# The first MLP product in written order with P3 in P2's banks, a new order of the out-projection chunks, and a norm by token rows

## The chip, the cores and the metric

One NeuronCore of a Trainium2 chip runs the whole program. The metric is the device time of one execution in microseconds (us), median of several runs.

## The reference

A decoder trunk of two layers over 1040 tokens (16 meta tokens and 1024 of the input), model width 1024, MLP width 4096, all in float32. Layer A: norm, stick-breaking attention, residual, norm, MLP with squared ReLU, residual. Then one shared key and value projection, and layer B with differential attention and the same kind of MLP. The part that the change touches is this, once in each layer:

```python
def rmsnorm(x, g):
    xf = x.astype(jnp.float32)
    y = xf * lax.rsqrt(jnp.mean(xf * xf, axis=-1, keepdims=True) + EPS)
    return (y * g.astype(jnp.float32)).astype(x.dtype)

def squared_relu_mlp(x, g, w_in, w_out):
    h = rmsnorm(x, g)
    return jnp.square(jax.nn.relu(h @ w_in)) @ w_out
...
            h = h + merge_heads(o) @ a_w_o[i]
...
        h = h + squared_relu_mlp(h, mlp_norm_g[layer], mlp_w_in[layer], mlp_w_out[layer])
```

## The kernel before

Activations stand with the model width on the partitions and tokens along the free dimension. Every float32 matmul is made of three: an operand is split by a cast (ScalarE) and a subtraction (VectorE) into a high and a low part, and high x high, high x low and low x high are added up in PSUM.

`mlp_stage` (line 732) runs once per layer (tag a, tag b; a letter at the end of a tile's name). It does four things.

**Out-projection and residual.** `step(m, v, k0)` makes row block m of the attention's output projection for one chunk v of tokens (tiles `opa`, weights `woa`), adds it to the residual (`hs[0]`, `hs[1]`, which are the two halves of the tokens, named `h0a` and `h1a`), squares it, and adds the square to the chunk's `acc`. The three chunks have 400, 384 and 256 tokens in layer a; the first lies in half 0, the last in half 1, the middle one in both. Blocks 0 to 2 come first for all chunks, then blocks 3 to 7 chunk by chunk, in the order 0, 1, 2.

**Norm.** `normed(v)` sums a chunk's `acc` over the partitions with one matmul by a matrix of ones (`rsa`), takes the root (ScalarE) and the RECIPROCAL (VectorE) on 128 rows that all hold the same, and scales the eight blocks.

**First product.** It is a seven-product scheme on 2 x 2 blocks. `ops7(c)` makes the seven operand blocks of half c (`put` is a cast and a subtraction of 128x1040 each), `w_split(u, i)` the seven weight blocks of unit u from raw weights `mwsa` (one sum, three differences s6, s7, s3, then cast and subtraction of 128x512 each). There are 16 units. `unit` runs P1 to P7, each of 24 matmuls of 260 columns (256 in layer b), 12 for each half; unit 0 is done in two parts, half 0 and then half 1. P1, P6, P7 and P4 use the PSUM buffer q1 in turn, P5 and P3 add up in q2, P2 has q3. Between products, sums are copied or added out (`u1a` to `u7a`, `ya`), squared ReLUs are taken, and the results are stored in `u_d`. Buffers come from a ring of four, three per unit, so q3 of a unit is the buffer that was q2 in the unit before.

```python
    PROD1 = (1, 5, 6, 2, 7, 3, 4)
...
                    q = {1: q1, 6: q1, 7: q1, 4: q1, 5: q2, 3: q2, 2: q3}[i]
...
                                mm(q[:, c, :nn], w[:, k], X7[c][i][:, y, k], k == 0 and wi == 0 and i in (1, 5, 2),
                                   k == 3 and wi == 2, skip_group_check=True)
...
                    elif i == 3:
                        tt(s(y12), b2, s(y12), ALU.add)
```

**Second product.** Seven passes of 16 steps read `u_d` and the output weights (tiles `moa`); each step makes two pairs of high and low parts (`waa`, `wba`) in the ring `wop`, which the weight pairs of the first product share. Behind it, between the layers, the stretch goes on with the projections of attention b (`bpj`), whose weights POOL scales (`bws`, line 1272).

What sets the order: a scheduler reorders the written instructions of every engine by its own simulation of their times, within the dependences, unless an instruction is pinned (`tc.keep_in_program_order`). So the order in which TensorE runs the products is not the written one. Line 159 is the matmul helper `mm`, 162 the transpose helper `tr`, 99, 105, 113 and 117 the helpers for casts, activations, two-operand and scalar-and-two-operand instructions.

Of the kernel before, what the change touches and what calls it, by code (L numbers as in the profile page):

```python
# [17 lines left out]
P = 128  # L18
# [60 lines left out]
def kernel(ctx: ExitStack, tc: tile.TileContext, inp, out):  # L79
# [78 lines left out]
    def mm(o, l, r, start, stop, **kw):  # L158
        nc.tensor.matmul(o, lhsT=l, rhs=r, start=start, stop=stop, **kw)  # L159

    def tr(o, i, ident):
        nc.tensor.transpose(out=o, in_=i, identity=ident)  # L162
# [565 lines left out]
    PROD1 = (1, 5, 6, 2, 7, 3, 4)  # L728
# [3 lines left out]
    def mlp_stage(li, WO, wo_src, wo_scale, O, views, kf, gcol, base, close_w, chunk_done, epilogue):  # L732
# [7 lines left out]
        st_h1, st_tp, st_h0 = ExitStack(), ExitStack(), ExitStack()  # L740
        hs = [None, pool(f"h1{tag}", stack=st_h1).tile([P, KT, half], F32, name=f"h1{tag}")]
        tp = pool(f"tp{tag}", stack=st_tp)
        accs = [tp.tile([P, 400], F32, tag="acc", bufs=3, name=f"acc{tag}_{c}") for c in range(3)]
        hs[0] = pool(f"h0{tag}", stack=st_h0).tile([P, KT, half], F32, name=f"h0{tag}")
# [7 lines left out]
        def wop(nm):  # L752
            return mw.tile([P, 2, 520], F32R, tag="wop", bufs=10, name=nm)
# [51 lines left out]

        def wo_load(m):
            ws = raw(f"wos{tag}_{m}").rearrange("p a b -> p (a b)").rearrange("p (k n) -> p k n", n=P)
            nc.sync.dma_start(out=ws, in_=wo_src[:, m * P:(m + 1) * P].rearrange("(k q) n -> q k n", q=P))
            W = []
            for k4 in range(2):  # L810
                w = wop(f"wo{tag}_{m}_{k4}")
                h, l = (w[:, i, :512].rearrange("p (k n) -> p k n", n=P) for i in range(2))
# [18 lines left out]
        def ops7(c):  # L831
# [4 lines left out]
            def tmp(nm):  # L836
                return wop(nm).bitcast(F32).rearrange("p a b -> p (a b)")[:, :4 * nn].rearrange("p (k n) -> p k n", n=nn)

            t3, t4 = (B12, B21) if not c else (tmp(f"t3{tag}"), tmp(f"t4{tag}"))
            return [lambda: put(c, 1, B11), lambda: tt(B11, B12, B11, ALU.subtract), lambda: put(c, 5, B11),  # L840
                    lambda: tt(t3, B22, B12, ALU.subtract), lambda: put(c, 3, B22), lambda: tt(B22, B22, B11, ALU.subtract),
                    lambda: put(c, 6, B22), lambda: put(c, 2, B21), lambda: tt(t4, B21, B22, ALU.subtract),
                    lambda: put(c, 7, t3), lambda: put(c, 4, t4)]
# [3 lines left out]

        for v in views:
            load_hs(v, 0, NMF)
        for m in range(NMF, KT):  # L850
            if m == NMF + 2:
                load_hs(views[0], NMF, KT)
            wo_load(m)
        for v in views[1:]:
            load_hs(v, NMF, KT)
# [3 lines left out]
        close_w()  # L859
        st_x = ExitStack()  # L860
        fa = pool(f"fa{tag}", stack=st_x, side="right")
        mc = pool(f"mc{tag}", stack=st_x, side="right")
# [32 lines left out]
        def unit(u, parts, more):  # L895
# [3 lines left out]
            U = {i: mc.tile([P, half], F32, tag="u", bufs=12, name=f"u{i}{tag}_{u}") for i in (1, 3, 5, 2, 4, 6, 7)}  # L899
            y12 = mc.tile([P, half], F32, tag="u", bufs=12, name=f"y{tag}_{u}")  # L900
            for pi, cs in enumerate(parts):
# [10 lines left out]

                for i in PROD1:
                    q = {1: q1, 6: q1, 7: q1, 4: q1, 5: q2, 3: q2, 2: q3}[i]
                    h, l = wops[u, i]
                    for k in range(4):
                        for wi, (w, y) in enumerate(((h, 0), (h, 1), (l, 0))):
                            for c in cs:
                                mm(q[:, c, :nn], w[:, k], X7[c][i][:, y, k], k == 0 and wi == 0 and i in (1, 5, 2),
                                   k == 3 and wi == 2, skip_group_check=True)  # L920
                    if i == 1:
                        acopy(s(U[1]), b1)
                    elif i == 6:
                        acopy(s(y12), b1)
                    elif i == 2:
                        tt(s(U[1]), b3, s(U[1]), ALU.add)
                        relu2(s(U[1]), s(U[1]))
                    elif i == 7:
                        acopy(s(U[3]), b1)
                        tt(s(U[3]), b2, s(U[3]), ALU.add)  # L930
                        relu2(s(U[3]), s(U[3]))
                    elif i == 3:
                        tt(s(y12), b2, s(y12), ALU.add)
                        relu2(s(y12), s(y12))
                        tt(s(U[5]), s(y12), s(U[1]), ALU.subtract)
                        tt(s(U[7]), s(U[3]), s(y12), ALU.subtract)
                        tt(s(U[6]), s(U[3]), s(U[5]), ALU.subtract)
                    elif i == 4:
                        relu2(s(U[2]), b1)
                        tt(s(U[4]), s(U[2]), s(U[6]), ALU.subtract)  # L940
                    if last_part and u + 1 < NPAIR:
                        w_split(u + 1, i)
                    more()
# [9 lines left out]
        x0, x1 = None, None  # L953
        for ci, v in enumerate(views):
            for m in range(NMF, KT):
                step(m, v, 0)
                if ci and m == NMF:
                    chunk_done(hs, ci - 1, ps1, srow)
                    normed(views[ci - 1])
                    if ci == 2:  # L960
                        w_load(0)
                        w_load(1)
                        x0, x1 = xact(0, 3, f"x0{tag}"), xact(1, 3, f"x1{tag}")
                        x2 = fa.tile([P, 2, 4, nn], F32R, name=f"x2{tag}")
# [595 lines left out]
```

## Time and profile before

| | |
|---|---|
| median of 3 runs | 2813.18 us (2811.96 to 2815.2) |
| profiled execution | 2817.75 us |
| its span | 2816.0 us |
| mean granted clock of TensorE | 0.979 |
| busy share: TensorE, VectorE, ScalarE, POOL | 94%, 71%, 54%, 12% |
| moved by DMA | 341.79 MB, 121 GB/s on average |

MLP a's first product runs from about 752 to 1109 us of the span and its second until 1440; in layer b they lie between 2134 and 2500, and from there to the end. Matmuls are pipelined: the records overlap, each shows about 0.28 us at 256 columns while one starts every 0.12 us. So a duration of a group of matmuls is read from the starts, not from the sum of the records. "[0.68 <-ACT u3a L99]" at a row's end means that the engine was idle for 0.68 us and that ScalarE's write of `u3a` (line 99) ended it.

### The profile page before, as it was taken

The numbers are of one execution on the slowest core, as the hardware profiler recorded it, in microseconds if no ns is written. First come the engines' busy times: TensorE is split into PE (matmuls) and PEld (weight loads), VectorE is DVE, ScalarE is ACT, GpSimd is POOL, SyncE is SP. The second block draws the span as 40 slices with busy tenths as digits, with TensorE's granted clock in tenths as the row PEclk, the third lists the DMA queues.
The fourth block names the chain that finished last, engine by engine and source line by source line (L and its number), as shares of the span: only waits on it lengthen the run. The fifth ranks groups of instructions, "written<-read, shape, count | busy, mean of one in ns | idle before, by whom it ended". The sixth has DMA issues, their size and how long they took to land.

```text
span 2816.0 us, 50084 instructions
## 1 busy us (share of the span) xinstructions
PE 2639.5 (94%) x18328; PEld 2487.6 (88%) x18328; DVE 1993.7 (71%) x3972; ACT 1513.0 (54%) x3543; POOL 335.2 (12%) x807
## 2 busy tenths in 40 slices
PE   7999999989799999899999999999897999999999
PEld 7889899978799999899999989999897999987887
DVE  6988999886955555665768878888768555457654
ACT  4666666664444444344556667667545444434443
POOL 2211111000000000000034334433000000000000
PEclk9999999999899999999999999999999999999999
DMA  7332233346143447733431112123352343495343
GB/s 209 93 82 78 78 80 80 105 137 188 44 148 128 141 144 271 249 100 103 133 86 47 39 53 57 50 58 113 102 172 94 131 142 134 159 340 165 94 109 116
DMA packets 298712, 341.79 MB, mean 121 GB/s; under 512 B 32537, under 2 KB 209346, under 8 KB 298466
## 3 DMA queue, kind: packets, MB, share of 16 engines
q1 hardware_dynamic: 289106, 334.32, 38.7%
q10 hardware_dynamic: 9360, 4.26, 0.6%
q8 instruction: 145, 2.38, 0.4%
q14 instruction: 101, 0.83, 0.1%
HBM read 206.99 MB, written 97.28 MB: 108 GB/s over the span
## 4 chain that ended last, share of the span: by engine, by line
PE 64%; DVE 11%; DMA 5%; ACT 4%; issue 2%; POOL 1%; SPq 1%; DVEq 0%; ACTq 0%; POOLq 0%
PE mia L159 11%; PE mib L159 11%; PE moa L159 10%; PE mob L159 9%; PE bpj L159 8%; PE sc_b L159 2%; PE pj L159 2%; DVE kp L494 2%; PE opb L159 2%; PE avb L159 2%; PE opa L159 1%; PE av L159 1%; PE ofb L159 1%; DVE wt L113 1%; PE ofa L159 1%
## 5 line engine op out<-in xcount | busy, mean ns | idle before, releaser
L159 PE MATMUL moa<-wba,waa 128*128 128x260 f32 x2688 | 326.7, 284 | 8.1 <-ACT wba L99 7.3
L159 PEld LDWEIGHTS moa<-wba,waa 128*128 128x128 f32 x2688 | 325.4, 189 | 9.1 <-ACT wba L99 7.7
L159 PE MATMUL mob<-wab,wbb 128*128 128x512 f32 x1344 | 316.1, 396 | 9.3 <-ACT wbb L99 7.0
L159 PEld LDWEIGHTS mob<-wab,wbb 128*128 128x128 f32 x1344 | 253.6, 189 | 70.5 <-ACT wbb L99 7.9
L159 PE MATMUL pj<-xa,wh 128*128 128x400 f32 (+2 forms) x1152 | 293.7, 334 | 8.0 <-DVE rsa L664 5.8
L159 PE MATMUL bpj<-bwh,xb 128*128 128x384 f32 x1024 | 283.0, 345 | 4.7 <-ACT k L99 3.7
L159 PEld LDWEIGHTS pj<-xa,wh 128*128 128x128 f32 x1152 | 204.0, 194 | 10.0 <-POOL ws L121 6.2
L159 PEld LDWEIGHTS bpj<-bwh,xb 128*128 128x128 f32 x1024 | 187.6, 190 | 8.2 <-ACT k L99 5.8
L494 DVE TENSOR_TENSOR_SCAN kp<-kp 128x144 f32<-128x144 f32 (+7 forms) x128 | 185.3, 1452 | 11.7 <-ACT kp L105 11.0
L159 PE MATMUL pj<-xa,wl 128*128 128x384 f32 (+2 forms) x576 | 191.5, 333 | 0.1
L159 PE MATMUL bpj<-bwl,xb 128*128 128x384 f32 x512 | 174.5, 341 | 0.0
L1272 POOL TENSOR_SCALAR bws<-bws,gains 128x128 f32<-128x128 f32 (+1 forms) x128 | 69.4, 548 | 824.5 <-DMA bws<-in_kv_w_dram 776.7
L105 ACT ACTIVATE w<-sc,rsa 128x392 f32<-128x392 f32 (+4 forms) x224 | 121.7, 544 | 33.6 <-PE sc L159 31.9
L105 ACT ACTIVATE kp<-sc,rsa 128x392 f32<-128x392 f32 (+4 forms) x224 | 120.3, 539 | 12.9 <-DVE w L113 12.8
L113 DVE TENSOR_TENSOR wt<-pt,wt 128x512 fp32r<-128x512 f32 x160 | 106.4, 681 | 23.4 <-ACT wt L99 22.8
L1331 DVE TENSOR_REDUCE mxb<-sc_b 128x1 f32<-128x144 f32 (+6 forms) x224 | 109.6, 503 | 18.0 <-PE sc_b L159 16.6
L99 ACT CAST wt<-pt 128x512 fp32r<-128x512 f32 x160 | 90.3, 587 | 56.9 <-PE av L159 51.6
L159 PE MATMUL av<-wt,v 128*128 128x256 f32 x640 | 109.7, 294 | 7.6 <-DVE wt L113 5.1
L159 PEld LDWEIGHTS pj<-xa,wl 128*128 128x128 f32 x576 | 111.5, 194 | 0.8 <-DVE wl L113 0.3
L113 DVE TENSOR_TENSOR w<-w,kp 128x143 f32<-128x143 f32 (+7 forms) x128 | 110.5, 868 | 2.0
L162 PE MATMUL pt<-cst,w 128*128 128x128 f32 x640 | 105.6, 279 | 5.3 <-DVE zm L113 2.7
L159 PEld LDWEIGHTS av<-wt,v 128*128 128x128 f32 x640 | 91.2, 193 | 12.0 <-DVE wt L113 7.0
(478 smaller groups left out, 7447.8 us busy)
## 6 DMA issues: line engine op xcount, KB each, us to landing
ba<-u_d SPq DMA_DIRECT2D x112, 260.0 KB, 2.7
bb<-u_d SPq DMA_DIRECT2D x112, 256.0 KB, 2.8
mwsa<-in_mlp_w_in_dram SPq DMA_DIRECT2D x32, 512.0 KB, 3.8
mwsb<-in_mlp_w_in_dram SPq DMA_DIRECT2D x32, 512.0 KB, 3.9
o_d<-oh SPq DMA_DIRECT2D x52, 256.0 KB, 2.5
ws<-in_a_w_qkv_dram SPq DMA_DIRECT2D x24, 512.0 KB, 4.2
qb<-q SPq DMA_DIRECT2D x128, 64.0 KB, 2.0
a12a<-in_mlp_w_out_dram SPq DMA_DIRECT2D x16, 512.0 KB, 4.1
```

Source lines behind the costliest of these rows:

```text
L99: nc.scalar.copy(out=o, in_=i)
L105: nc.scalar.activation(out=o, in_=i, func=func, **kw)
L113: nc.vector.tensor_tensor(out=o, in0=a, in1=b, op=op)
L159: nc.tensor.matmul(o, lhsT=l, rhs=r, start=start, stop=stop, **kw)
L162: nc.tensor.transpose(out=o, in_=i, identity=ident)
L494: nc.vector.tensor_tensor_scan(out=rv, data0=rv, data1=rv, initial=1.0, op0=ALU.mult, op1=ALU.bypass)
L1272: nc.gpsimd.tensor_scalar(out=ws[:, s], in0=ws[:, s], scalar1=gains[:, gc + k:gc + k + 1], scalar2=1.0, op0=ALU.mult, op1=ALU.mult)
L1331: nc.vector.tensor_reduce(out=mx[:, j:j + 1], in_=ps[:, 0], axis=AX.X, op=ALU.max, negate=True)
```

## The change

1. `mm`, `tr` return their instruction, and `pin` keeps one in program order. The first matmul of every product is pinned. In units 1 to 15 the order is 1, 5, 6, 2, 7, 3, 4 as before in the text; in unit 0 it is 1, 2, 5, 3, 6, 7, 4, and half 1 comes first.
2. P3 starts its own sum in q3, after P2's was read out, so `y12` takes two additions: P5 from q2, P3 from q3.
3. The chunks go in the order 1, 2, 0. Half 1's blocks are made during chunk 0; chunk 0's norm and half 0's blocks are written inside unit 0's first part (`second`).
4. The raw weights of units 0 and 1 are loaded and the seven splits of unit 0 are written ahead of the chunks.
5. The norm works on token rows: `rms_of` sums with `acc` as weights, so that 128 tokens stand on the partitions and each group of 128 tokens is a column; the root and RECIPROCAL act on at most four columns; `normed` transposes the factors, broadcast to 128, into PSUM (`rba`), from where the scaling reads them.
6. Memory: `wop` has 8 buffers instead of 10 and moves to a pool that lives to the end of the second product, and the weights of the out-projection have a ring of their own with five buffers, which some operand blocks use afterwards; `u` has 10 instead of 12. The weights of attention b take the place of `wop`.

```diff
-        def normed(v):
+        def rms_of(v):
 
             c, off, n = v
-            r = tp.tile([P, 400], F32, tag="r", bufs=1, name=f"r{tag}{c}")[:, :n]
             ps = ps1(f"rs{tag}{c}")
-            mm(ps[:, :n], ones, accs[c][:, :n], True, True)
-            act(r, ps[:, :n], AF.Sqrt, scale=1.0 / D, bias=epst)
-            nc.vector.reciprocal(out=r, in_=r)
+            r = tp.tile([P, 4], F32, tag="r", bufs=3, name=f"r{tag}{c}")
+            nf, rem = divmod(n, P)
+            for i in range(nf + (rem > 0)):
+                w = P if i < nf else rem
+                ins = mm(ps[:w, 2 * i:2 * i + 2], accs[c][:, P * i:P * i + w], ones[:, 0:2], i == 0, i == nf + (rem > 0) - 1,
+                         skip_group_check=True)
+                if i == 0:
+                    pin(ins)
+            for w, i, k in [(P, 0, nf)] + ([(rem, nf, 1)] if rem else []):
+                act(r[:w, i:i + k], ps[:w, 2 * i:2 * (i + k):2], AF.Sqrt, scale=1.0 / D, bias=epst[:w])
+                nc.vector.reciprocal(out=r[:w, i:i + k], in_=r[:w, i:i + k])
+            return r
+
+        def normed(v, r):
+
+            c, off, n = v
+            ps = ps1(f"rb{tag}{c}")
+            for o in range(0, n, P):
+                w = min(P, n - o)
+                ins = tr(ps[:, o:o + w], r[:w, o // P:o // P + 1].to_broadcast([w, P]), idf[:w, :w])
+                if o == 0:
+                    pin(ins)
             for x, a, b, w in pieces(v):
                 for k in range(KT):
                     hv = hs[x][:, k, a:a + w]
-                    stt(hv, hv, gains[:, gcol + k:gcol + k + 1], r[:, b:b + w], ALU.mult, ALU.mult)
+                    stt(hv, hv, gains[:, gcol + k:gcol + k + 1], ps[:, b:b + w], ALU.mult, ALU.mult)
...
-                for i in PROD1:
-                    q = {1: q1, 6: q1, 7: q1, 4: q1, 5: q2, 3: q2, 2: q3}[i]
+                done = set()
+                for pn, i in enumerate(prods):
+                    q = {1: q1, 6: q1, 7: q1, 4: q1, 5: q2, 3: q3, 2: q3}[i]
...
-                                mm(q[:, c, :nn], w[:, k], X7[c][i][:, y, k], k == 0 and wi == 0 and i in (1, 5, 2),
-                                   k == 3 and wi == 2, skip_group_check=True)
+                                ins = mm(q[:, c, :nn], w[:, k], X7[c][i][:, y, k], k == 0 and wi == 0 and i in (1, 5, 2, 3),
+                                         k == 3 and wi == 2, skip_group_check=True)
+                                if k == 0 and wi == 0 and c == cs[0]:
+                                    pin(ins)
...
+                    if now(6, 5):
+                        tt(s(y12), b2, s(y12), ALU.add)
...
-                    elif i == 3:
-                        tt(s(y12), b2, s(y12), ALU.add)
+                    if now(6, 5, 3):
+                        tt(s(y12), b3, s(y12), ALU.add)
...
+        w_load(0)
+        w_load(1)
+        for i in PROD1:
+            w_split(0, i)
+
+        for ci, v in enumerate(order):
             for m in range(NMF, KT):
                 step(m, v, 0)
                 if ci and m == NMF:
-                    chunk_done(hs, ci - 1, ps1, srow)
-                    normed(views[ci - 1])
+                    chunk_done(hs, order[ci - 1], ps1, srow)
+                    r = rms_of(order[ci - 1])
+                if ci and m == NMF + 1:
+                    normed(order[ci - 1], r)
                     if ci == 2:
...
+        def second(pi, pn):
+
+            nonlocal todo
+            if pi:
+                return
+            if pn == 1:
+                late["r"] = rms_of(order[2])
+            elif pn == 2:
+                normed(order[2], late["r"])
...
+            elif pn > 2:
+                work(3)
+
+        unit(0, ((1,), (0,)), PROD0, second)
```

How it moves instructions, at three places. First **TensorE in unit 3 of layer a**, at the ends of its last products. A row is a line, the operation, the PSUM tile (`mia_3_0_0` is unit 3's q1, `_1` q2, `_2` q3) and the operands (`w7a_3` is the weight block of P7). Before:

```order
L159 MATMUL mia_3_0_0_10005<-x5a_9343,w7a_3_9918 128x260
L159 MATMUL mia_3_0_0_10005<-x2a_9052,w4a_3_9983 128x260
...
L159 MATMUL mia_3_0_0_10005<-x5a_9343,w4a_3_9983 128x260
L159 MATMUL mia_3_0_1_10006<-x1a_9051,w3a_3_9953 128x260
...
L159 MATMUL mia_3_0_1_10006<-x4a_9238,w3a_3_9953 128x260
L159 MATMUL mia_4_0_2_10243<-x1a_9051,w2a_4_10121 128x260
```

And now:

```order
L159 MATMUL mia_3_0_2_10027<-xaa_9113,w2a_3_9905 128x260
L159 MATMUL mia_3_0_0_10025<-y7a_9311,w7a_3_9938 128x260
...
L159 MATMUL mia_3_0_0_10025<-x7a_9218,w7a_3_9938 128x260
L159 MATMUL mia_3_0_2_10027<-y3a_9309,w3a_3_9973 128x260
...
L159 MATMUL mia_3_0_2_10027<-xba_9114,w3a_3_9973 128x260
L159 MATMUL mia_3_0_0_10025<-xda_9315,w4a_3_10003 128x260
...
L159 MATMUL mia_3_0_0_10025<-x4a_9219,w4a_3_10003 128x260
L159 MATMUL mia_4_0_0_10262<-xca_9308,w1a_4_10053 128x260
```

P4 no longer comes directly behind P7, nor P2 of the next unit behind P3; P3 writes q3, and unit 4 begins with its P1.

Second **TensorE at the handover of layer a**, from the last chunk's out-projection into unit 0. Before:

```order
L159 MATMUL opa_2_7_9152<-oa2_7586,woa_7_0_8522 128x256 x12
L159 MATMUL opa_2_7_9152<-oa2_7586,woa_7_1_8525 128x256 x12
L159 MATMUL rsa2_9199<-acca_2_8478,ones_66 128x256
L159 MATMUL mia_0_0_0_9253<-x0a_9050,w1a_0_9186 128x260 x12
L159 MATMUL mia_0_0_1_9254<-x0a_9050,w5a_0_9193 128x260 x12
L159 MATMUL mia_0_0_2_9255<-x1a_9051,w2a_0_9218 128x260 x12
L159 MATMUL mia_0_0_0_9253<-x0a_9050,w6a_0_9215 128x260 x12
L159 MATMUL mia_0_1_0_9381<-x3a_9237,w1a_0_9186 128x260 x12
L159 MATMUL mia_0_0_0_9253<-x1a_9051,w7a_0_9223 128x260 x12
L159 MATMUL mia_0_1_1_9382<-x3a_9237,w5a_0_9193 128x260
```

And now:

```order
L159 MATMUL opa_0_7_9185<-oa0_7055,woa_7_8522 128x400 x24
L159 MATMUL mia_0_0_0_9241<-xaa_9113,w1a_0_8656 128x260 x12
L159 MATMUL mia_0_0_2_9243<-xaa_9113,w2a_0_8668 128x260 x12
L159 MATMUL rsa0_9272<-ones_66,acca_0_8479 128x2 x3
L159 MATMUL rsa0_9272<-ones_66,acca_0_8479 16x2
L159 MATMUL mia_0_0_1_9242<-xaa_9113,w5a_0_8660 128x260 x12
L162 MATMUL rba0_9294<-cst_60,ra0_9273 128x128 x3
L162 MATMUL rba0_9294<-cst_60,ra0_9273 128x16
L159 MATMUL mia_0_0_2_9243<-xba_9114,w3a_0_8678 128x260 x12
L159 MATMUL mia_0_0_0_9241<-xba_9114,w6a_0_8665 128x260 x12
L159 MATMUL mia_0_0_0_9241<-x7a_9218,w7a_0_8673 128x260 x12
L159 MATMUL mia_0_0_0_9241<-x4a_9219,w4a_0_8681 128x260 x12
```

The norm of the last chunk stood ahead of the first product and now stands inside it, behind P2; its transposes (`rba0`) stand behind P5.

Third **VectorE in the out-projection of layer a, now**, after chunk 1's last row block but one:

```order
L113 TENSOR_TENSOR woa_7_8522<-wosa_7_8520,woa_7_8522 128x512 x2
L113 TENSOR_TENSOR w1a_0_8656<-mwsa_0_0_8648,w1a_0_8656 128x512
L113 TENSOR_TENSOR mwsa_0_0_8648<-mwsa_0_0_8648,mwsa_0_1_8650 128x4x128
...
L113 TENSOR_TENSOR w4a_0_8681<-mwsa_0_1_8650,w4a_0_8681 128x512
L113 TENSOR_TENSOR mwsa_1_0_8652<-mwsa_1_0_8652,mwsa_1_1_8654 128x4x128
L113 TENSOR_TENSOR w1a_1_9413<-mwsa_1_0_8652,w1a_1_9413 128x512
L113 TENSOR_TENSOR acca_1_8480<-acca_1_8480,sqa_1_7_0_8851 128x120
L113 TENSOR_TENSOR acca_1_8480<-acca_1_8480,sqa_1_7_1_8856 128x264
```

The splits of the weights of unit 0 and the first of unit 1 stand ahead of the last additions into chunk 1's `acca_1`, on which its norm waits; before, they stood behind all of that chunk's additions.

## Rows read from the trace of the kernel before

**Rows 1.** The page: the span, and TensorE's busy time and share.
```profile
span 2816.0 us, 50084 instructions
...
PE 2639.5 (94%) x18328; PEld 2487.6 (88%) x18328; DVE 1993.7 (71%) x3972; ACT 1513.0 (54%) x3543; POOL 335.2 (12%) x807
```

**Rows 2.** Stretches: busy time (instructions) by engine, granted clock, DMA share, GB/s.
```profile
740.00:752.00 12.00, 0.95 (x3) 0.84 (x3) 12.00 (x16) 3.59 (x4) 0.00 (x0) 0.50 0.19 59
751.71:776.31 24.60, 23.20 (x171) 22.20 (x169) 24.38 (x35) 16.86 (x34) 0.00 (x0) 0.93 0.10 33
800.00:1075.00 275.00, 258.11 (x2104) 253.37 (x2104) 145.12 (x222) 133.23 (x226) 0.00 (x0) 1.00 0.40 138
1125.00:1140.00 15.00, 9.21 (x77) 8.99 (x75) 4.08 (x7) 0.00 (x0) 0.00 (x0) 0.92 1.07 377
1260.00:1310.00 50.00, 50.00 (x418) 50.00 (x417) 31.01 (x53) 20.68 (x36) 0.00 (x0) 1.00 0.38 103
2133.67:2161.50 27.83, 23.29 (x169) 22.01 (x168) 27.39 (x40) 15.57 (x30) 0.00 (x0) 0.93 0.15 48
```

**Rows 3.** Waits of TensorE, 752 to 1100: us in total, times, longest.
```profile
PE mia L159 <- DVE ya L113: 11.0, 13, 1.6
PE mia L159 <- ACT u3a L99: 8.2, 12, 0.7
```

**Rows 4.** Waits of TensorE, 2134 to 2490, same columns.
```profile
PE mib L159 <- DVE yb L113: 11.4, 13, 2.0
```

**Rows 5.** Timeline of TensorE in layer a: start, duration, instruction [wait and releaser].
```profile
859.74 0.28 PE L159 MATMUL mia<-x5a,w7a 128*128 128x260 f32 x1
860.71 0.39 PE L159 MATMUL mia<-x2a,w4a 128*128 128x260 f32 x1 [0.68 <-ACT u3a L99]
...
867.52 0.39 PE L159 MATMUL mia<-x1a,w2a 128*128 128x260 f32 x1 [0.79 <-DVE ya L113]
...
870.52 0.28 PE L159 MATMUL mia<-x0a,w1a 128*128 128x260 f32 x1
...
873.39 0.28 PE L159 MATMUL mia<-x0a,w6a 128*128 128x260 f32 x1
...
882.84 0.39 PE L159 MATMUL mia<-x2a,w4a 128*128 128x260 f32 x1 [0.68 <-ACT u3a L99]
```

**Rows 6.** Timeline of ScalarE in the same unit.
```profile
860.06 0.59 ACT L99 COPY u3a<-mia 128x520 f32<-128x520 f32 x1 [2.26 <-PE mia L159]
```

**Rows 7.** Timeline of TensorE at the two handovers.
```profile
751.05 1.22 PE L159 MATMUL rsa<-acca,ones 128*128 128x256 f32 x2 [15.33 <-DVE acca L113]
...
2133.04 1.19 PE L159 MATMUL rsb<-accb,ones 128*128 128x256 f32 x2 [11.67 <-DVE accb L113]
```

**Rows 8.** Timeline of TensorE in layer b: the fourth product of two units.
```profile
2441.28 0.39 PE L159 MATMUL mib<-x2b,w4b 128*128 128x256 f32 x1 [0.68 <-ACT u3b L99]
...
2463.10 0.39 PE L159 MATMUL mib<-x2b,w4b 128*128 128x256 f32 x1 [0.68 <-ACT u3b L99]
```

**Rows 9.** Instructions of VectorE by line, 800 to 1075: busy us, mean ns | idle before.
```profile
L113 DVE TENSOR_TENSOR u7a<-u3a,ya 128x520 f32<-128x520 f32 x13 | 9.0, 694 | 0.0
L113 DVE TENSOR_TENSOR u1a<-mia,u1a 128x520 f32<-128x520 f32 x13 | 9.0, 693 | 1.4 <-issue 1.4
```

**Rows 10.** Timeline of TensorE, then of VectorE, in the out-projection of layer a.
```profile
691.66 8.83 PE L159 MATMUL opa<-oa,woa 128*128 128x400 f32 x48 [0.84 <-ACT woa L99]
...
723.95 11.78 PE L159 MATMUL opa<-oa,woa 128*128 128x256 f32 x96
...
700.92 0.69 DVE L113 TENSOR_TENSOR mwsa<-mwsa,mwsa 128x512 f32<-128x512 f32 x1 [0.53 <-DMA mwsa<-in_mlp_w_in_dram]
```

**Rows 11.** Timeline of POOL, then of TensorE, between MLP a and attention b.
```profile
1438.06 0.48 POOL L1272 TENSOR_SCALAR bws<-bws,gains 128x256 f32<-128x256 f32 x1 [0.75 <-DMA bws<-in_kv_w_dram]
...
1445.16 3.38 PE L159 MATMUL rsx<-ones,accx 128*128 128x2 f32 x16 [5.41 <-DVE accx L113]
1449.05 0.42 PE L159 MATMUL bpj<-bwh,xm 128*48 128x256 f32 x1 [0.51 <-DVE nx L117]
```

More of the change, by code (lines that the diff above doesn't have):

```diff
@@ L158, in mm, with pin @@
     def mm(o, l, r, start, stop, **kw):
-        nc.tensor.matmul(o, lhsT=l, rhs=r, start=start, stop=stop, **kw)
+        return nc.tensor.matmul(o, lhsT=l, rhs=r, start=start, stop=stop, **kw)
     def tr(o, i, ident):
-        nc.tensor.transpose(out=o, in_=i, identity=ident)
+        return nc.tensor.transpose(out=o, in_=i, identity=ident)
+    def pin(ins):
+        tc.keep_in_program_order(ins)
     const = pool("const")
@@ L851, in mlp_stage @@
             if m == NMF + 2:
-                load_hs(views[0], NMF, KT)
+                load_hs(order[0], NMF, KT)
             wo_load(m)
-        for v in views[1:]:
+        for v in order[1:]:
             load_hs(v, NMF, KT)
@@ L893, in w_split, with unit @@
             wops[u, i] = h, l
-        def unit(u, parts, more):
+        def unit(u, parts, prods, more):
             if u + 2 < NPAIR:
                 w_load(u + 2)
-            U = {i: mc.tile([P, half], F32, tag="u", bufs=12, name=f"u{i}{tag}_{u}") for i in (1, 3, 5, 2, 4, 6, 7)}
-            y12 = mc.tile([P, half], F32, tag="u", bufs=12, name=f"y{tag}_{u}")
+            mc = late["mc"]
+            U = {i: mc.tile([P, half], F32, tag="u", bufs=10, name=f"u{i}{tag}_{u}") for i in (1, 3, 5, 2, 4, 6, 7)}
+            y12 = mc.tile([P, half], F32, tag="u", bufs=10, name=f"y{tag}_{u}")
             for pi, cs in enumerate(parts):
@@ L967, in mlp_stage @@
                 if ci == 2 and m > NMF:
                     work(2)
[L969 to L971 removed]
+        X7[1] |= {i: xblk(f"x{i}{tag}") for i in (7, 4)}
         work(99)
[L973 to L980 removed]
@@ L981, in mlp_stage @@
-        X7[1] = {1: xa[:, 0], 5: xa[:, 1], 3: xb[:, 0], 6: xb[:, 1], 2: xb[:, 2]}
-        todo = ops7(1)
-        def last_blocks():
-            st_h1.close()
-            xc = pool(f"fc{tag}", stack=st_x, side="right").tile([P, 2, 2, 4, nn], F32R, name=f"x5{tag}")
-            X7[1] |= {7: xc[:, 0], 4: xc[:, 1]}
-        todo.insert(9, last_blocks)
-        unit(0, ((0,), (1,)), lambda: work(2))
+        st_h1.close()
+        late["mc"] = pool(f"mc{tag}", stack=st_x, side="right")
+        chunk_done(hs, order[2], ps1, srow)
@@ new lines, in second @@
+        def second(pi, pn):
[6 more added lines that the diff above has]
+                normed(order[2], late["r"])
+                st_tp.close()
+                xc = xact(0, 3, f"xc{tag}")
+                X7[0] = {1: xc[:, 0], 2: xc[:, 1], 5: xc[:, 2]} | {i: xblk(f"y{i}{tag}") for i in (3, 6, 7)}
+                X7[0][4] = pool(f"fb{tag}", stack=st_x, side="right").tile([P, 2, 4, nn], F32R, name=f"xd{tag}")
+                todo = ops7(0)
+            elif pn > 2:
+                work(3)
@@ L991, in mlp_stage @@
+        unit(0, ((1,), (0,)), PROD0, second)
+        st_h0.close()
         for u in range(1, NPAIR):
-            unit(u, ((0, 1),), lambda: None)
+            unit(u, ((0, 1),), PROD1, lambda *a: None)
         st_x.close()
+        st_wo.close()
         st_h, st_q = ExitStack(), ExitStack()
@@ L1086, in mlp_stage @@
         st_q.close()
+        st_w.close()
         st_h.close()
@@ L1508, with to_rows @@
         head_out(HB - 1, 3, O)
[L1511 to L1513 removed]
+    def to_rows(hs, v, ps1, srow):
+        c, off, n = v
         t0 = CH[c][0] + off - NM
```

79 lines of the change are left out of this document (33 added, 46 removed).

## Prediction

> **What bounds the kernel now.** I read the page's busy shares first. TensorE is busy 94% of the span [rows 1], which looks like a kernel with nothing left to take. But a mean over 2816 us hides stages, so next I cut the span into stretches. In the middle of layer a's first MLP product TensorE is busy 258.11 of 275 us, at a granted clock of 1.00, with VectorE and ScalarE near half busy; in an undisturbed piece of the second product it is busy 50.00 of 50.00 [rows 2]. So the first product loses time with no engine full. The list of waits says on what: thirteen waits for VectorE's `ya` and twelve for ScalarE's `u3a` in layer a, and thirteen for `yb` in layer b [rows 3, 4]. One of each per unit is a pattern of the order, not an accident. The timeline shows it: product 1 (P1; the seven are named P1 to P7) starts at 870.52 and product 6 at 873.39, so an undisturbed product of 24 matmuls takes 2.87 us; but the fourth product of one unit starts at 860.71 and that of the next at 882.84, a pitch of 22.13, where seven products would need 7 x 2.87 = 20.09 [rows 5]. **2.04 us per unit** are lost. Its two places are P4, which follows P7 in the same banks and waits till ScalarE has copied P7's sum out, and P2 of the next unit, which follows P3 directly in the buffer that VectorE must first read for `ya` [rows 5, 6]. Before the first unit stands the other loss: TensorE waits 15.33 us in layer a and 11.67 in layer b with the norm's sum at the head of its queue [rows 7], while VectorE is busy 12.00 of 12.00 [rows 2].
>
> **The change, part by part.** The sum is made against the profiled execution, span 2816.0 [rows 1], 2817.75 with what lies around it; the median of the runs, 2813.18, is 4.57 below that.
>
> *Written order and P3's banks.* The order of the instructions now has 1, 5, 6, 2, 7, 3, 4 in each of the units 1 to 15. Between P7 and P4 stands P3. The copy of P7 takes 0.59 us [rows 6]; between P7's last matmul and P4's first TensorE now has 2.87 us of other work, where the gap from the one to the other was 0.97 (859.74 to 860.71, [rows 5]). P2 of the next unit comes four products after P3. I looked at every other reuse of a bank: the shortest is P5 of the next unit in the banks that the ReLU of U2 reads, one product behind P4, against some 0.6 us for a ReLU of the copy's shape [rows 6]. So both waits go and none takes their place; a unit costs 20.09. Layer b's pitch is 21.82 [rows 8]; its products have 256 of 260 columns, 20.09 x 256/260 = 19.78, so it loses 2.04 too. The waits listed as ended by `ya` are thirteen in each layer; 13 x 2.04 = **26.5 us** in each, 53 in both. What is added is one VectorE addition per unit (y12 now takes P5 and P3 separately): 0.69 us [rows 9] x 31 = 21 us of busy time, under a VectorE that is busy 145.12 of 275 us [rows 2]. It costs nothing; if VectorE were full, it would cost these 0.69 us of each unit's 20.09, a third of the gain.
>
> *Norm by token rows.* Three RECIPROCALs on up to 400 columns per layer leave VectorE for ones on at most four columns. TensorE gets nine matmuls of two columns (0.21 us each, from 3.38 us for sixteen of that form after the MLP, [rows 11]) and nine transposes of at most 128 columns, no longer each; the three wide sums go. That is some +2 us per layer, held in the handover's times below. Each scaling now reads its factor from PSUM instead of SBUF. The trace prices that: an addition of 128x520 that reads PSUM takes 693 ns and one that reads SBUF alone 694 [rows 9], so nothing. The Trainium skill, page "Perfetto Trace Analysis", section "Optimizing Scalar/DVE Operations", gives VectorE about 65 ns more per instruction on PSUM than on SBUF, which would make the 32 scalings of a layer 2 us dearer; the rows here do not bear it out.
>
> *The handover from attention to MLP.* Before, VectorE had to norm the last chunk and make blocks of half 0 ahead of the first product, and all seven weight splits fell into the same stretch. Now the chunks come in the order 1, 2, 0, half 1's blocks are made under the last chunk's out-projection, half 0's during the first part of unit 0. Gone are at most the 15.33 and 11.67 us [rows 7]; that is one bound. The other is that the time comes back in new waits, and the order of the instructions shows three. (i) `woa_7` is reached sooner, since the first chunk has 384 columns and not 400, while its cast still ends the wait at 691.66 [rows 10]: the wait of 0.84 grows to about 2.8. (ii) VectorE's last additions into chunk 1's squares now stand behind the seven splits of unit 0 and the sum and first split of unit 1; that sum waited for its load until 700.92 [rows 10]. With that sum, a split (0.69 each) and the additions, the norm's matmul can go at 703 to 706, while TensorE, which has 46 matmuls left to do after 691.66 (96 short ones took 11.78, [rows 10]; the longer ones among the 46 add one), stands there from about 698.6: 5 to 8 us, I take 7, and all of the out-projection's rest is pushed by it. (iii) In unit 0 the pinned norm matmul waits some 2 us for the last chunk's squares, and P7 and P4 of the first part wait for ScalarE's copies, which stand behind casts of 128x1040. Layer a: the out-projection ended near 751.05 - 15.33 = 735.7 [rows 7]; 735.7 + 7.1 = 742.8 is when unit 0 starts, against 751.71. Unit 0 then takes its 20.1 and about 11 us of waits (2 for the norm, the rest for copies and for half 0's blocks, which VectorE and ScalarE need in a row), done at 773.9; before, its 168 matmuls were done at 776.3 [rows 2]. That is **2.4 us** gained where 15 looked free. Layer b, by the same steps: the stall before its first norm is about 5.5 and the out-projection ended near 2133.04 - 11.67 = 2121.4 [rows 7], less a part that the transposes ahead hide; unit 0 starts at 2126.3 against 2133.67, and is done near 2154.7 against 2161.5 [rows 2]: **6.8 us**.
>
> *Buffers.* Weight pairs have 8 buffers instead of 10. In the first product each is refilled one product after its last use, as long as before the seven weights of a unit need; nothing. In the second product a step (24 matmuls, or 12 of twice the columns in layer b) takes two buffers, so the lead falls from five steps to four, 11.5 to 8.6 us beyond the running one; a step's inputs need a load, a cast and a subtraction (the last two 0.6 to 0.7 each), and the undisturbed stretch shows no wait at all [rows 2]. I take 1 us per layer, for one shorter lead after each burst; bounds 0 and 5. Where the second product starts, TensorE is starved by loads today already (9.21 of 15 us, at 377 GB/s, [rows 2]). These loads go out when the last unit frees its blocks, so they move forward with it; the order of the frees changes, -4 to +4 us per layer, I take 0. Between the layers, the weights of attention b now land in memory that the second product's pairs held; before, POOL was scaling the last of them at 1438.06, eleven microseconds ahead of the first projection at 1449.05 [rows 11]. That cover mostly goes: with half of it as the upper bound, 0 to 5.5, I take +2.5 us.
>
> **Sum:** 26.5 + 26.5 + 2.4 + 6.8 - 2 - 2.5 = **57.7 us**. From the span that is 2758.3; from the median, 2813.2 - 57.7 = 2755.5, so **2756 us**.
>
> **Rivals.**
> 1. *The handovers close as well.* If VectorE's additions do not wait for the second load and unit 0's copies slip between the casts, the two idle stretches go whole: 15.3 + 11.7 + 53 - 4.5 = 75.5, or 2738. For it: VectorE's full stretch before TensorE's wait is what the change thins. Against: the order that it now stands in.
> 2. *The wait moves.* P5 of the next unit waits for the ReLU of U2, since ScalarE runs its casts in a queue and that ReLU could stand behind one or two of 0.6 us; or the pinned products wait for late splits that the free order could walk around. With one wait like P4's of 0.97 us per unit left, 30 units x 0.97 = 29 of the gain are gone: 2785. That the change does not do what it says is the same case taken twice (all of it back, 2813); the order of the instructions shows products 1 to 7 as written, so I give it hardly anything.
> 3. *Slower: the second product starves.* With 8 buffers a step waits if load, cast and subtraction together take longer than 8.6 us. There are 2 x 112 steps (7 passes of 16 in each layer). The gain of 57.7 is gone at 57.7/224 = 0.26 us per step, and the kernel is slower by over 0.2% at 0.28. If every second step waited as long as the gap seen at P4, 0.97 us, it would be 112 x 0.97 = 109 us: 2756 + 109 = 2865. Against it stands 50.00 of 50.00 with two buffers more.
>
> **How the numbers follow.** 0.2%, about 5.6 us, is what a measurement of this kernel can tell from no change. The forecast has 0.70, rival 1 0.13, rival 2 0.09 (0.01 of it with nothing left), rival 3 0.04; the other 0.04 is a mix of lesser losses (burst, weights of attention b, handovers slower than before) that leaves 10 to 40 us. All but rival 3, the dead change and a part of the mix are faster: 0.93. Same 0.03, slower 0.04. The range takes in rival 1 with the burst's better bound in one layer, 2738 - 4, and reaches nearly to rival 2, past the worse bounds of buffers, burst and the weights of attention b (2756 + 8 + 8 + 3 = 2775): 2733 to 2782.
>
> **What will show it.** Right: the stretch of the first product has TensorE busy over 99%, the pitch from one fourth product to the next is 20.1 and 19.8, and neither `ya` nor `u3a` is among its waits. Unit 0: waits for the norm and for ScalarE's copies in both layers, with the first product some 8 us earlier and unit 1 only a few. Wrong, if waits for `u2a` stand once per unit, if the second product's undisturbed stretch shows TensorE idle with a pair's subtraction as the releaser, or if the first projection of attention b comes later after the MLP's end by more than 5 us.

## The result: faster, by half of what was forecast

The changed kernel takes 2785.9 us (median of 4, 2780.3 to 2790.5) where the kernel before takes 2814.1: ratio 0.990, 95% interval 0.9878 to 0.9921. That is 28 us, or 34 from one profiled span to the other (2816.0 to 2781.6), where 57.7 were forecast; it lies above the range.

The page of the changed kernel, as [rows 1] of before:

```profile
span 2781.6 us, 50340 instructions
...
PE 2635.3 (95%) x18367; PEld 2495.0 (90%) x18367; DVE 1997.8 (72%) x4007; ACT 1515.7 (54%) x3544; POOL 327.1 (12%) x807
```

Stretches of the changed kernel (columns as in [rows 2]): the middle of the first product; the out-projection behind its new wait; unit 0; the begin of the second product; an undisturbed piece of it.

```profile
800.00:1050.00 250.00, 250.00 (x2085) 250.00 (x2085) 150.03 (x232) 131.89 (x221) 0.00 (x0) 1.00 0.43 149
702.50:708.50 6.00, 5.95 (x28) 5.98 (x29) 4.07 (x8) 1.56 (x3) 0.00 (x0) 0.50 0.21 71
740.50:776.00 35.50, 26.53 (x181) 24.89 (x180) 30.85 (x48) 19.77 (x37) 0.00 (x0) 0.86 0.10 33
1079.00:1145.00 66.00, 51.83 (x387) 51.02 (x386) 34.91 (x57) 19.07 (x34) 0.00 (x0) 0.87 1.00 364
1260.00:1310.00 50.00, 50.00 (x418) 50.00 (x418) 28.07 (x50) 21.69 (x40) 0.00 (x0) 1.00 0.39 105
```

The first row is the steady state without a gap: 250.00 of 250.00, where before it was 258.11 of 275. The losses are in the three rows behind it. TensorE's timeline names what ended them, in the out-projection, in unit 0 (three rows), at the begin of the second product (two rows) and between the layers:

```profile
702.55 0.78 PE L159 MATMUL rsa<-ones,acca 128*128 128x2 f32 x3 [5.85 <-DVE acca L113]
...
744.88 0.96 PE L159 MATMUL rsa<-ones,acca 128*128 128x2 f32 x8 [1.28 <-DVE acca L113]
...
752.99 1.70 PE L159 MATMUL mia<-x7a,w7a 128*128 128x260 f32 x12 [0.46 <-ACT ya L99]
...
759.42 2.97 PE L159 MATMUL mia<-x4a,w4a 128*128 128x260 f32 x12 [4.73 <-ACT u3a L99]
...
1111.00 5.00 PE L159 MATMUL moa<-wba,waa 128*128 128x260 f32 x24 [9.17 <-ACT wba L99]
...
1133.05 1.23 PE L159 MATMUL moa<-wba,waa 128*128 128x260 f32 x4 [4.13 <-ACT wba L99]
...
1434.49 0.45 PE L159 MATMUL bpj<-bwh,xm 128*48 128x256 f32 x1 [3.27 <-POOL xm L124]
```

To see where time went, I cut both spans at starts of TensorE's matmuls and did the same with every experiment. "handover" is from the first out-projection matmul with weights `woa` (`wob` in layer b) to the first P1; "unit 0" its 168 matmuls; "units 1-15" to the last matmul of the first product, less second-product matmuls mixed in (36 of 0.12 us in layer a and 58 of 0.236 in layer b before, 4 in each layer of the changed kernel); "first pass" from there to the 385th matmul of the second product (193rd in layer b), those mixed in added; "between" from the last of the second product to the first projection; "attention b" from the first to the last projection. Each column is one profiled execution. The rest of a span, most of it ahead of the first out-projection, is not listed; it takes from 759.3 us (changed) to 772.6 (e8), so up to 13 us between two columns' spans can come from there.

```
us             before changed      e1      e2      e3      e4      e5      e6      e8      e9     e10     e11
handover a       79.0    71.3    78.9    70.4    71.2    70.6    71.2    78.7    78.7    78.8    78.9    79.3
unit 0 a         24.5    35.5    25.3    37.6    32.2    35.9    39.3    25.3    25.4    25.4    24.6    22.8
units 1-15 a    328.9   302.4   302.0   302.4   329.7   302.4   302.4   328.0   301.9   301.9   325.6   302.1
first pass a     56.9    66.0    59.8    46.3    64.3    65.2    46.2    47.2    46.2    46.2    59.4    59.8
passes 2-7 a    277.4   277.0   276.0   277.1   276.4   276.8   277.1   278.3   276.5   276.5   276.8   277.0
between           9.7    13.0     9.7    13.1    13.3    13.0    13.1     9.7     9.7     9.7     9.8     9.1
attention b     521.2   526.2   522.5   526.3   526.0   525.6   526.0   521.4   525.7   520.1   522.3   523.9
handover b       77.9    66.6    78.1    66.7    66.7    70.5    66.7    78.1    78.0    66.7    77.9    77.9
unit 0 b         27.9    34.1    32.5    33.1    29.7    31.3    38.6    27.8    33.3    31.1    29.7    26.0
units 1-15 b    324.9   298.1   297.7   298.1   325.3   298.1   298.1   322.2   298.0   298.1   320.7   298.8
first pass b     52.2    62.5    57.2    44.6    55.8    61.2    44.6    47.1    44.7    44.6    47.1    58.9
passes 2-7 b    272.4   269.6   271.0   271.3   270.3   269.6   270.9   271.5   271.4   272.1   274.3   270.6
span           2816.0  2781.6  2776.5  2747.7  2823.7  2781.9  2758.4  2797.0  2762.1  2735.4  2810.3  2772.6
```

Before to changed: the units give 26.4 and 26.8 us, as forecast. The first passes take back 9.1 and 10.2. Handover and unit 0 together lose 3.4 in layer a (79.0 + 24.5 against 71.3 + 35.5) and gain 5.1 in layer b. The stretch between the layers takes back 3.3, attention b 5.0; passes 2 to 7 give 0.4 and 2.8.

### The profile page after: what moved, and what is told of

Read it like the earlier page. It is cut to its first block, busy times and chain, and to the rows that moved or that the text cites. A ratio compares the mean times of both kernels' runs of the same rounds, so it can differ in the third digit from the quotient of the medians.

```text
span 2781.6 us, 50340 instructions
## 1 busy us (share of the span) xinstructions
PE 2635.3 (95%) x18367; PEld 2495.0 (90%) x18367; DVE 1997.8 (72%) x4007; ACT 1515.7 (54%) x3544; POOL 327.1 (12%) x807
## 5 line engine op out<-in xcount | busy, mean ns | idle before, releaser
L159 PE MATMUL moa<-wba,waa 128*128 128x260 f32 x2688 | 329.4, 286 | 14.2 <-ACT wba L99 14.2
L105 ACT ACTIVATE w<-sc,rsa 128x392 f32<-128x392 f32 (+4 forms) x224 | 121.4, 543 | 33.1 <-PE sc L159 31.6
L105 ACT ACTIVATE kp<-sc,rsa 128x392 f32<-128x392 f32 (+4 forms) x224 | 120.1, 538 | 13.3 <-DVE w L113 13.2
```

The lines of the kernel that those rows point to most:

```text
L105: nc.scalar.activation(out=o, in_=i, func=func, **kw)
L159: return nc.tensor.matmul(o, lhsT=l, rhs=r, start=start, stop=stop, **kw)
```

## The experiments

The theory after the result had two parts: the loads for the second product come in such an order that they starve its first pass, and the new handover exchanges one wait for several. Rivals: the bytes themselves are the bound; the memory layout or the held order makes the first pass dear; VectorE's work bounds unit 0 whatever the order.

### e1_units_only: the held order and the banks alone

```diff
--- before
-                    q = {1: q1, 6: q1, 7: q1, 4: q1, 5: q2, 3: q2, 2: q3}[i]
+                    q = {1: q1, 6: q1, 7: q1, 4: q1, 5: q2, 3: q3, 2: q3}[i]
...
+                                if u and k == 0 and wi == 0 and c == cs[0]:
+                                    tc.keep_in_program_order(ins)
...
+                        tt(s(y12), b2, s(y12), ALU.add)
...
-                        tt(s(y12), b2, s(y12), ALU.add)
+                        tt(s(y12), b3, s(y12), ALU.add)
```

> Of the change this has only the held order of units 1 to 15 and P3 in q3; memory, chunks and norm are as before. Both theories: the sixteen units lose their 2.04 us each, so units 1 to 15 take 302 us in layer a where before they took 329. Theory A (the held order itself frees the operand blocks late, so the loads for the second product start later against its begin): the first pass of the second product takes 62 us or more where before it took 57, and the span is about 2816 - 53 + 10 = 2773. Theory B (the new memory layout does it): the first passes take 57 and 52 us as before, span 2763. Attention b between its first and last projection takes 521 us as before if the changed kernel's 526 come from its new place in memory, and 526 if they come from elsewhere.

Measured: 2778.6 us, ratio 0.986 (0.983 to 0.9887). The units take what they take in the whole change; the first passes take 59.8 and 57.2, between the two theories. So neither theory holds alone: this edit and the rest of the change each add a part. That it is the held order that makes the first pass dear, as theory A has it, is not borne out: e11 below has 59.8 and 58.9 without the held order. And these few lines of the diff are worth as much as the whole of it.

### e3_free_units: the whole change without the held order and with P3 in q2

```diff
--- changed
+                    q = {1: q1, 6: q1, 7: q1, 4: q1, 5: q2, 3: q2 if u else q3, 2: q3}[i]
...
-                                if k == 0 and wi == 0 and c == cs[0]:
+                                if not u and k == 0 and wi == 0 and c == cs[0]:
...
```

> The whole change but the held order in units 1 to 15, where P3 adds up in q2 again as before. Both theories: the two waits per unit are back, units 1 to 15 take about 329 us in layer a. Theory A (the held order makes the first pass dear): first passes about 57 and 52 us, span 2782 + 53 - 18 = 2817. Theory B (the layout): first passes stay at 66 and 62, span 2835. The handover and unit 0 do not change (71 and 35.5 us in layer a).

Measured: 2824.6 us, ratio 1.0026 (1.001 to 1.0042): without the units' part the change makes the kernel slightly slower. The two waits per unit are back (329.7 and 325.3). The first passes, 64.3 and 55.8, again fit neither theory alone: in layer a it is mostly the layout, in layer b more e1's edit. Unit 0 of layer a was expected to stay at 35.5 and took 32.2; why is not known.

### e2_loads_in_order: what the two have in common

```diff
--- changed
...
-                    nc.sync.dma_start(out=H[:, 4 * mh:4 * mh + 4, s], in_=h_d[:, 4 * mh:4 * mh + 4, s])
+                    pin(nc.sync.dma_start(out=H[:, 4 * mh:4 * mh + 4, s], in_=h_d[:, 4 * mh:4 * mh + 4, s]))
...
-            nc.sync.dma_start(out=t, in_=wr[max(k, 0), :, f0:f0 + 4, c0:c0 + 512])
+            pin(nc.sync.dma_start(out=t, in_=wr[max(k, 0), :, f0:f0 + 4, c0:c0 + 512]))
```

(and the same for layer b's loads from `y_d`.)

> The whole change, and the loads of the output weights and of the residual for the second product are held at the place in the queue where they are written, between the steps' own inputs. Theory: those loads, issued early and in a row, stand ahead of the first pass's own inputs in the issuing queue and on the DMA engines; held back, the first pass falls from 66 to about 50 us in layer a and from 62 to about 50 in layer b, span about 2782 - 28 = 2754. Rival (the bytes are the bound whatever their order): first and second pass together take as long as in the changed kernel, within 3 us.

Measured: 2750.7 us, ratio 0.9761 (0.9735 to 0.9786); the first passes take 46.3 and 44.6, no more than later passes (46.2 each in layer a), and passes 2 to 7 grow by at most 1.7 us. The queue shows why. SyncE's queue in the changed kernel, while TensorE does the first steps of the second product (start, time in the queue, transfer):

```profile
1079.17 2.39 SPq L1091 DMA_DIRECT2D ba<-u_d  x1
1081.65 0.77 SPq L1062 DMA_DIRECT2D ra2a<-in_mlp_w_out_dram  x1
1082.52 2.59 SPq L979 DMA_DIRECT2D u_d<-u3a  x1
1085.16 0.58 SPq L1062 DMA_DIRECT2D ra2a<-in_mlp_w_out_dram  x1
1085.83 2.26 SPq L1095 DMA_DIRECT2D a12a<-in_mlp_w_out_dram  x1
1088.14 8.00 SPq L1058 DMA_DIRECT2D hqa<-h_d  x4
1096.24 2.10 SPq L979 DMA_DIRECT2D u_d<-u5a  x1
1098.39 0.44 SPq L1058 DMA_DIRECT2D hqa<-h_d  x1
...
1102.62 0.32 SPq L1091 DMA_DIRECT2D ba<-u_d  x1
```

Between two loads of a step's input (`ba`) pass 23.5 us, more than eight steps of 2.87; TensorE runs dry at 1101.8 and waits till 1111.00. What stands between are stores, residual blocks (`hqa`) that the pass's end or later ones want, weights (`ra2a`) that no step of this pass reads, and one load of weights that its steps do read (`a12a`). The same stretch of the queue with the loads in order, and TensorE's stretch over the first pass:

```profile
1078.57 0.32 SPq L1091 DMA_DIRECT2D ba<-u_d  x1
...
1084.85 1.51 SPq L1091 DMA_DIRECT2D ba<-u_d  x1
...
1089.02 0.32 SPq L1091 DMA_DIRECT2D ba<-u_d  x1
...
1093.78 1.65 SPq L1091 DMA_DIRECT2D ba<-u_d  x1
```

```profile
1080.00:1127.00 47.00, 47.00 (x394) 47.00 (x393) 26.93 (x44) 19.91 (x35) 0.00 (x0) 1.00 1.02 374
```

The DMA engines are as full there (1.02, 374 GB/s) as in the changed kernel's stretch above (1.00, 364 GB/s), and TensorE is busy 47.00 of 47.00. From 1079 to 1145 either kernel moves the same bytes (24.06 MB, and 24.16 in order), but with 16 loads of `ba` and 8 of `hqa` in the changed kernel, 19 and 4 in order. So the bytes are not the bound; their order is. The rival falls: first pass and passes 2 to 7 together take 323.4 us instead of 343.0 in layer a.

### e6_before_loads and e8_units_loads: the same edit without the change

e6 is the kernel before with e2's edit; e8 has e1's and e2's edits.

> The kernel before, unchanged but for the second product's loads in written order. Theory: the loss at the second product's begin was there before and has nothing to do with the products' order; the first passes fall from 57 to 46 us and from 52 to 45, span 2816 - 18 = 2798, units as before. Rival: only the changed kernel's loads come too early; nothing moves, span 2816.

> The kernel before with two edits alone: held order of units 1 to 15 with P3 in q3, and the second product's loads in written order; memory, chunks and norm as before. Theory: both gains add, 2776.5 - 13.5 - 12.5 = span 2750, first passes 46 and 45 us; the other parts of the change together (chunk order, early splits, norm by rows, memory) are then worth within 5 us of nothing, since the kernel with all of them has 2748. Rival: those parts are worth 10 us or more, which the loads had hidden; then this one stays above 2758.

Measured: e6 2800.8 us, ratio 0.9958 (0.9942 to 0.9974), first passes 47.2 and 47.1; the loss was there before the change. e8 2757.7 us, ratio 0.9794 (0.9777 to 0.981), first passes 46.2 and 44.7. Against e2's 2750.7 the medians leave 7 us for the other parts of the change, but the two intervals overlap. The profiled span of e8, 2762.1, lies in the rival's range, above 2758; yet it is the slowest of its four executions, and 772.6 us of it lie outside the listed stages, against 760.7 in e2. By stage they are worth: layer a 104.1 against 108.0 for handover and unit 0 (they cost 4), layer b 111.3 against 99.8 (they give 11.5), between the layers 9.7 against 13.1 (they cost 3.4). That is some 4 us in all, so the stages speak for the theory; the times alone don't decide it.

### e10_order_only and e11_banks_only: which half of the units' gain

e10 is e1 with P3 left in q2, e11 is e1 without the two lines that hold the order.

> The kernel before with the held order of units 1 to 15 alone; P3 still adds up in q2 behind P5. Theory (the banks carry the gain, the order alone doesn't): P3 now follows P7 directly and must wait until U3 is added out of q2, a copy and an addition behind P7's end, some 1.7 us, so units 1 to 15 take about 302 + 15 x 1.7 = 327 us in layer a, as before. Rival (the order carries it): about 302.

> The kernel before with P3 in q3 and its two additions alone; the scheduler orders the products freely. Theory (the banks carry the gain): it finds an order without the two waits, units 1 to 15 take under 306 us in layer a. Rival (without the held order the products are again put where a copy is waited for): over 315 us.

Measured, one execution each: e10 2812.1 us, e11 2774.4. TensorE between 800 and 1050, the list of waits of e10 and the stretch of e11:

```profile
PE mia L159 <- DVE u3a L113: 17.0, 12, 1.4
```

```profile
800.00:1050.00 250.00, 250.00 (x2089) 250.00 (x2088) 146.60 (x231) 131.54 (x224) 0.00 (x0) 1.00 0.45 150
```

With the order alone, P3 waits for the addition out of q2 behind P7, once per unit, and 325.6 us are left of 328.9. With the banks alone the scheduler finds an order without a wait by itself (302.1). P3's bank is the gain; the held order adds nothing to it (298.8 with the banks alone in layer b, 298.1 in the changed kernel).

### e4_splits_later: the wait ahead of the first norm

```diff
--- changed
-        for i in PROD1:
-            w_split(0, i)
...
                     r = rms_of(order[ci - 1])
+                    if ci == 1:
+                        for i in PROD1:
+                            w_split(0, i)
```

with the subtractions of unit 0's splits, and the first sums of units 0 and 1, pinned on VectorE.

> The whole change, but the splits of unit 0's weights stand behind chunk 1's last additions on VectorE. Theory: the wait of 5.85 us ahead of the first norm in layer a goes, and with it the stretch at the lower clock behind it (28 matmuls at 0.214 us apart), so unit 0 begins about 8 us earlier; in layer b nothing, since there was no such wait. Whether the span falls by these 8 depends on unit 0: if VectorE's blocks of half 0 bound it, it gets longer by part of them (span 2774 to 2782); rival: the splits, now late, make unit 0's first products wait and nothing is gained.

Measured: 2789.0 us, ratio 0.9893 (0.9867 to 0.9918): nothing. TensorE's timeline in e4:

```profile
700.22 0.80 PE L159 MATMUL rsa<-ones,acca 128*128 128x2 f32 x6 [1.68 <-DVE acca L113]
...
720.80 0.61 PE L159 MATMUL rsa<-ones,acca 128*128 128x2 f32 x4 [1.53 <-DVE acca L113]
```

The wait of 5.85 us shrank to 1.68, but a second one stands ahead of the next norm, and the handover is 0.7 us shorter, not 8. The lower clock did not go either. In three stretches of the out-projection (columns as in [rows 2]) the granted clock is 0.50 with TensorE busy throughout, the first behind a wait of 2.19 us for `woa`, the others behind the two above:

```profile
691.10:694.40 3.30, 3.30 (x17) 3.30 (x16) 0.00 (x0) 0.62 (x1) 0.00 (x0) 0.50 1.03 338
701.30:704.60 3.30, 3.30 (x18) 3.30 (x17) 2.90 (x6) 1.76 (x5) 0.00 (x0) 0.50 0.00 0
721.80:725.10 3.30, 3.30 (x12) 3.26 (x11) 0.10 (x1) 0.00 (x0) 0.00 (x0) 0.50 0.00 0
```

In layer b, where nothing was expected, the handover grew from 66.6 to 70.5 us and unit 0 fell from 34.1 to 31.3. That pinned splits push other VectorE work back is my reading; no run isolates it.

### e5_copies_first: P4's wait in unit 0

```diff
--- e2
-            acopy(d[:, 0], src)
+            ins = nc.scalar.copy(out=d[:, 0], in_=src)
+            if not c:
+                pin(ins)
...
-            elif pn > 2:
-                work(3)
+            elif pn > 4:
+                work(99 if pn == 6 else 3)
```

> The kernel with the loads in written order (span 2747.7), and in unit 0 ScalarE's casts for half 0's blocks pinned behind its copies of P6's and P7's sums. Theory: P4 waits 5 us because its copy stands behind casts that wait for VectorE; so that wait and the stretch at the lower clock behind it go, unit 0 falls from 37.6 to about 32 us in layer a and from 33.1 to about 28 in layer b, span about 2738. Rival: VectorE's norm and blocks of half 0 are the bound, the wait comes back ahead of the second part's products, and unit 0 stays within 1.5 us.

Measured: 2758.6 us, ratio 0.9805 (0.979 to 0.9819), 8 us slower than e2. P4's wait is gone, and the second part's products wait one by one:

```profile
759.93 1.71 PE L159 MATMUL mia<-x4a,w4a 128*128 128x260 f32 x12 [0.47 <-ACT u3a L99]
...
763.60 1.59 PE L159 MATMUL mia<-xca,w1a 128*128 128x260 f32 x11 [0.89 <-DVE xca L113]
...
769.15 2.75 PE L159 MATMUL mia<-xca,w5a 128*128 128x260 f32 x11 [1.63 <-DVE xca L113]
...
775.27 0.39 PE L159 MATMUL mia<-y6a,w6a 128*128 128x260 f32 x1 [1.67 <-ACT y6a L856]
```

Unit 0 takes 39.3 instead of 37.6 us, in layer b 38.6 instead of 33.1. The rival's waits came, but not its number (within 1.5 us), and the run doesn't show that half 0's blocks bound unit 0 without this edit: the edit itself makes them later. VectorE's first subtraction for one (`xca`) starts 17.0 us behind the first P1, in e2 13.3. What is shown is an exchange: casts behind the copies end P4's wait and make the second part wait for blocks. What bounds unit 0 stays open.

### e9_mixed: the best of the stages

Layer a as in e8, layer b as in e2.

> Layer a as in the kernel before, with the held order, P3 in q3 and the second product's loads in written order; layer b as the whole change with its loads in written order. By the stages measured so far: handover and unit 0 of layer a 104 us against 108 with the whole change there, of layer b 100 against 111 with the old one, between the layers 9.7 us against 13.1. Theory (the stages add): span about 2748 - 4 - 3.4 = 2740. Rival (the stages are not independent, what is won early is waited for later): not below 2747.

Measured: 2736.7 us, ratio 0.9721 (0.9696 to 0.9746), below both kernels and all other runs. The span, 2735.4, is what the sum said within 5 us, partly by luck. Against e2's 2747.7 the two stages of the sum gave what they should (3.8 and 3.4 us); attention b gave 6.2 and unit 0 of layer b 2.0, which the sum did not hold, and the unlisted stretches took 3.5 back.

## Why the prediction was wrong, point by point

**The units** were right: 2.04 us times thirteen, 26.5 us, against 26.4 and 26.8 measured, and TensorE 250.00 of 250.00. From one P4 to the next the middle units take 20.2 and 19.9 us, forecast 20.1 and 19.8. The added VectorE addition costs nothing. The mechanism I gave it needs a correction: not order and banks together, but the banks (e10, e11). The Trainium skill, page "Perfetto Trace Analysis", section "Optimization Strategy", says that the same gap repeating on the engine that should be saturated can mean that there isn't enough SBUF or PSUM for the next tile. In this case the gaps were waits for a PSUM buffer, but not for want of buffers: in e11 moving P3 to another of the same ring ended both (250.00 of 250.00), with none added.

**The step that failed** is "These loads go out when the last unit frees its blocks, so they move forward with it; the order of the frees changes, -4 to +4 us per layer, I take 0." It measured +9.1 and +10.2. Both the bounds and their reason were wrong. I read the starved stretch at 377 GB/s [rows 2] as a limit of bytes that no order changes, and bounded the change by how far frees move. It was a limit of order: loads wanted later stood in the queue ahead of those wanted next (the rows under e2). That they stand there because the scheduler issues a load as soon as its memory is free is my reading, not shown. Edits to memory or order reshuffle that queue: over the seven kernels without e2's edit the first pass takes 56.9 to 66.0 us in layer a and 47.1 to 62.5 in layer b (e10 even wins 5 us there). So its price was unbounded by the row I used. The row with the same bandwidth and a busy TensorE came only with e2.

**The handover** was right in layer a's waits and wrong in a size. Forecast in layer a: 2.8 us for `woa_7` (2.7 measured), 7 ahead of the first norm (5.85 measured), 2 at the last (1.28), then P4 behind casts (4.73); 2.4 us gained. Measured: 3.4 lost. The out-projection's start-to-P1 gained 7.7, of 8.9 forecast, but unit 0 took 35.5 instead of 31.1. Its waits are not the reason: TensorE is idle for 9.0 of the 35.5 us, where 11 were forecast, but busy for 26.5 where 20.1 were. The missing term, for the most part, is the clock (0.86 on average there). Behind a wait of some 5 us the granted clock was 0.50, the lower level of 1.2 GHz: in the stretch 702.5 to 708.5, 28 matmuls took 6 us, 0.214 apart, where 256 columns otherwise take 0.12; behind P4's wait, at 759.42, twelve took 2.97 where P7's twelve took 1.70 (752.99). The waits lost their own length and then two microseconds or so each. Layer b gained 5.1 of the 6.8 forecast, and that is luck: the wait of 5.5 us ahead of its first norm did not come, so the handover gained 11.3 where 7.4 were forecast, and unit 0 lost 6.2 where 0.6 were.

**Between the layers** +3.3 for +2.5 taken: right, with POOL's `xm` as the releaser that the weights' late scaling holds up; POOL in the changed kernel:

```profile
1429.27 2.94 POOL L1314 TENSOR_SCALAR bws<-bws,gains 128x256 f32<-128x256 f32 x5 [3.82 <-DMA bws<-in_kv_w_dram]
...
1433.74 0.69 POOL L124 TENSOR_SCALAR xm<-xb 128x128 fp32r<-128x128 f32 x2
```

**The smaller ring** was put at 1 us per layer and costs nothing: passes 2 to 7 take 277.0 us in layer a, 277.4 before. Rival 3 is out. **The norm's factor in PSUM** costs nothing either, as the rows of the kernel before said [rows 9]; scaling before (from SBUF) and after (from PSUM):

```profile
L117 DVE SCALAR_TENSOR_TENSOR h0a<-h0a,gains,ra 128x400 f32<-128x400 f32 x8 | 4.5, 630 | 0.0
```

```profile
L117 DVE SCALAR_TENSOR_TENSOR h0a<-h0a,gains,rba 128x400 f32<-128x400 f32 x8 | 4.4, 626 | 2.4 <-PE rba L162 2.4
```

**Attention b** took 5.0 us longer, which no term held. Its place in memory was my guess, and e8 speaks against it: it has the old memory and 525.7, while e1, with the same, has 522.5 and e9, whose weights of attention b also land where they did before, 520.1. One profiled execution per kernel can't tell a cause from variation here; this stays open.

Of the three numbered rivals, none came. For the first (the handovers close whole) the idle time ahead of unit 0 did go, but other waits, there and in unit 0, took its place. The second has the measured time, 2785, but by chance: its wait in every unit isn't there (250.00 of 250.00). What came is the mix of lesser losses, burst first, that leaves 10 to 40 us; I gave it 0.04. My signs of being wrong did not include the begin of the second product, where the largest loss was.

## What to carry to other kernels

A stretch where the DMA engines are full is not yet bound by bytes: look in the issuing queue at what stands between two loads of the next step's input, and hold loads that are wanted later at their written place. Where a product waits once per round for its accumulator to be read out, give it another of the buffers that are free then, before fixing any order. When a change thins the work ahead of a wait, find where the same engine is needed next, and price the slow clock behind each new wait along with the wait.

## What the runs showed of the hardware that I had not expected

Full DMA engines and a full TensorE go together: 374 GB/s at a busy share of 1.02 with TensorE busy 47.00 of 47.00 (e2), and 364 GB/s with TensorE waiting 14.2 us in three waits (the changed kernel). And a TensorE stall that is short against the whole costs more than itself: after 5.85 us of waiting, the granted clock was at 0.50 for the next 6 us.
